# A DeltaNet stage under a list scheduler: 64x64 products of the merges staggered by head, booked times and the order of projections replaced

## The chip, the cores and the metric

The kernel runs on one core of a Trainium2 chip, in one launch. The metric is the device time of the launch in microseconds; a run of the kernel is told as the median of its executions with the lowest and the highest beside it. All arithmetic is in float32. The large products of the dense work are split by the kernel into three products of rounded parts (high times high, low times high, high times low).

## The reference, cut to what matters

The network has two layers on a sequence of 1024 positions of width 1024. The change lies wholly in the first of them, a gated DeltaNet with 8 heads of 128 and chunks of 64:

```python
q, k, v = chunks(q), chunks(k), chunks(v)
gcum = jnp.cumsum(chunks(g[..., None])[..., 0], axis=-1)
decay = jnp.where(causal, jnp.exp(jnp.where(causal, diff, 0.0)), 0.0)
m = jnp.where(strict, jnp.einsum("bhnid,bhnjd->bhnij", k_beta, k) * decay, 0.0)
uw = lax.linalg.triangular_solve(m + eye, rhs, left_side=True, lower=True, unit_diagonal=True)
...
def step(state, inp):
    v_new = u_c - jnp.einsum("bhcd,bhdv->bhcv", w_c, state)
    o_c = jnp.einsum("bhcd,bhdv->bhcv", qd, state) + jnp.einsum("bhcj,bhjv->bhcv", a_c, v_new)
    state = state * dec[..., None, None] + jnp.einsum("bhcd,bhcv->bhdv", ke, v_new)
```

Around it stand the projection of the normed input to q, k, v and the gate z (each 1024 wide), a causal convolution of width 4 with silu on q, k and v, and the output projection with the residual. After it come a gated convolutional FFN, a chunked attention layer and a second FFN.

## The kernel before

**The dense work.** The four projections are 32 tiles of 128 output columns, each for two halves of the sequence (512 positions). One half of one tile is 8 units, and one unit is three matmuls of 128x128 weights on 512 columns, written in `dense` (lines 118, 119 and 120), which accumulate in one PSUM tile `acc`. The output projection is 16 more halves of 8 units (`acco`). A tile's weights come by one DMA (`raw_tile`, line 571) and are split into high and low parts on ScalarE and GpSimd (`split_tile`). After each half `project` takes the convolution's taps on ScalarE and VectorE and silu on ScalarE and GpSimd.

**The recurrence between it.** While TensorE works through the units, the kernel puts the small work of the DeltaNet between them, for the heads in four groups t = 0..3 (heads 0-3 and 4-7 of the first half, then of the second). The kernel works on pairs of chunks, so its blocks are 128x128. `gram` makes k times k (`pg`, line 712) and the masked matrix `mn`; `invert_blocks` inverts its small diagonal blocks on VectorE; `merge` (two calls for each t, each for two heads with four blocks each) puts the inverse of the 128x128 blocks together from them; `prep` makes transposes of k and v and the product `pqk`; `chain` carries the state from block to block (lines 926, 930, 939 on TensorE, a step on VectorE or ScalarE after each), `output` (903, 904) makes the output of a block, `qnorm` takes the sums of squares of q (transposes `pq`, line 655, then four squares on ScalarE, line 659), and `finish` with `turn` or `turn_last` norms and turns the result (`po`, lines 985 and 1032).

**The merge, step by step.** On TensorE a merge before the change is six groups of small products on one PSUM tile `pm` of 128 partitions by 8 by 64 columns: 32 products of 32x32 (line 845), 32 more (851), 16 (862), 24 (872 and 874), then 8 products of 64x64 that write the lower 64 partitions (881), and 8 products of 64x64 that write the upper 64 partitions (886). Between them stand copies on ScalarE or VectorE, among them the copy of `pm` into `TY` after 881 (line 883) and into the inverse `U` after 886 (line 888), each of 64 partitions by 512. The 8 products are four blocks of each of the two heads.

**What sets the order.** TensorE's, VectorE's and ScalarE's instructions stand in the order in which the program text issues them, and class `Flow` decides that order while the kernel is built. Each piece of small work is a generator that yields the booked time from which its next step may be issued. `Flow.T` is a booked clock of TensorE: `pe(n, dt)` adds the booked time of small products, one unit adds 0.69. `on(engine, cost)` books work on VectorE ("D"), ScalarE ("A") or GpSimd ("G") and gives the time at which it is booked to be done. `Flow.run` issues the first ready item by rank whose time plus `slack` (0.5) has passed on the booked clock, and one unit of dense work where there is none. `bank` hands out the two PSUM tiles of the pool `paux` (two buffers), in which `pg`, `pq`, `pk`, `pqk`, `pv`, `pu` and `po` stand in turn: the third user has to wait until the first one has been read out. The list `ORDER` names the sequence in which the tiles of k, q and v are projected. No booked number is in the program that runs; the numbers only decide which instruction follows which.

## Time and profile before

| what | value |
|---|---|
| three executions | 2499.27 us median (2497.41 to 2501.43) |
| profiled execution, span from the first to the last instruction | 2493.3 us |
| granted TensorE clock | 1.000 of full speed |
| TensorE matmul busy, whole span | 2466.1 us (99%), 13785 matmul records |
| VectorE / ScalarE / GpSimd busy | 74% / 58% / 61% |
| the DeltaNet stage with its output projection | about 0 to 671 us of the span |

The profiled execution is known by its span; 6.0 us lie between that span and the median of the three executions, which were timed from outside. A float32 matmul of 128 or fewer columns in the small work stands in the trace as two records, a transposition as one, so "x16" for the 64x64 products is eight products. Records of matmuls overlap (a matmul of 512 columns reads 0.39 us and the next one starts 0.23 us after it), so the time that TensorE gives to a matmul is read from the chain of waits or from the starts in the timeline, not from the busy time. The matmuls' line numbers are those of the kernel before; in the changed kernel most lines lie 3 or 18 lower down.

### The profile page before, as it was taken

The numbers are of one execution on the slowest core, as the hardware profiler recorded it, in microseconds if no ns is written. First come the engines' busy times: TensorE is split into PE (matmuls) and PEld (weight loads), VectorE is DVE, ScalarE is ACT, GpSimd is POOL, SyncE is SP. The second block draws the span as 40 slices with busy tenths as digits, with TensorE's granted clock in tenths as the row PEclk, the third lists the DMA queues.
The fourth block names the chain that finished last, engine by engine and source line by source line (L and its number), as shares of the span: only waits on it lengthen the run. The fifth ranks groups of instructions, "written<-read, shape, count | busy, mean of one in ns | idle before, by whom it ended". The sixth has DMA issues, their size and how long they took to land.

```text
span 2493.3 us, 39279 instructions
## 1 busy us (share of the span) xinstructions
PE 2466.1 (99%) x13785; PEld 2057.0 (83%) x13785; DVE 1842.5 (74%) x2985; ACT 1442.1 (58%) x2770; POOL 1523.0 (61%) x1548
## 2 busy tenths in 40 slices
PE   8999999999999999999999999999999999999998
PEld 6888888888888888888788888888877888888877
DVE  5665874567798888888866656666589788888886
ACT  6444546474465556565555666667456565666555
POOL 3655653357357777777626454455554777778774
PEclk9999999999999999999999999999999999999999
DMA  8734435565347777777841232333444799777788
GB/s 228 188 105 118 142 110 153 156 194 163 96 108 148 150 153 151 153 144 156 183 151 55 67 80 77 81 76 95 145 114 119 184 176 180 166 169 171 152 187 224
DMA packets 383877, 353.19 MB, mean 142 GB/s; under 512 B 97600, under 2 KB 304448, under 8 KB 383680
## 3 DMA queue, kind: packets, MB, share of 16 engines
q1 hardware_dynamic: 350704, 243.46, 34.4%
q0 software_dynamic: 28224, 98.58, 22.5%
q10 hardware_dynamic: 4752, 8.65, 0.9%
q8 instruction: 108, 1.77, 0.3%
q14 instruction: 89, 0.73, 0.1%
HBM read 182.25 MB, written 156.30 MB: 136 GB/s over the span
## 4 chain that ended last, share of the span: by engine, by line
PE 81%; POOL 6%; DVE 4%; issue 4%; DMA 2%; ACT 2%; SPq 0%; ACTq 0%; POOLq 0%; DVEq 0%
PE acc L118 8%; PE pu L1448 8%; PE acc L119 8%; PE acc L120 8%; PE pu L1446 8%; PE pu L1447 8%; PE pd L1448 3%; PE pd L1446 3%; PE pd L1447 3%; POOL ul L1412 3%; PE acco L118 2%; PE acco L120 2%; PE acco L119 2%; PE ptp L2353 2%; PE poT L2399 1%
## 5 line engine op out<-in xcount | busy, mean ns | idle before, releaser
L1412 POOL TENSOR_TENSOR ul<-r,uh 128x512 fp32r<-128x512 f32 x266 | 430.4, 1638 | 258.3 <-ACT uh L1434 253.5
L118 PE MATMUL acc<-xh,whi 128*128 128x512 f32 x896 | 369.3, 413 | 0.5 <-ACT xh L1094 0.5
L119 PE MATMUL acc<-xl,whi 128*128 128x512 f32 x896 | 352.1, 393 | 0.4 <-POOL xl L381 0.3
L120 PE MATMUL acc<-xh,wlo 128*128 128x512 f32 x896 | 351.3, 392 | 0.0
L103 POOL TENSOR_TENSOR wlo<-wraw,whi 128x256 fp32r<-128x256 f32 (+1 forms) x326 | 237.0, 758 | 107.8 <-ACT whi L101 105.3
L1434 ACT CAST uh<-r 128x512 fp32r<-128x512 f32 x289 | 177.1, 623 | 183.3 <-DVE r L1412 148.8
L1448 PE MATMUL pu<-xh,ul 128*128 128x512 f32 x524 | 204.4, 390 | 0.7 <-POOL ul L1412 0.7
L1446 PE MATMUL pu<-xh,uh 128*128 128x512 f32 x524 | 204.4, 390 | 0.7 <-ACT keep L1575 0.7
L1802 ACT COPY stage<-pd 128x1024 f32<-128x1024 f32 x180 | 175.3, 1014 | 49.7 <-PE pd L1448 48.8
L1447 PE MATMUL pu<-xl,uh 128*128 128x512 f32 x524 | 203.9, 389 | 0.0
L120 PEld LDWEIGHTS acc<-xh,wlo 128*128 128x128 f32 x896 | 168.5, 188 | 37.1
L2308 POOL TENSOR_SCALAR sS<-sS,st 128x640 f32<-128x640 f32 (+4 forms) x128 | 87.6, 691 | 178.4 <-DVE st L2306 168.2
L119 PEld LDWEIGHTS acc<-xl,whi 128*128 128x128 f32 x896 | 169.3, 189 | 28.4 <-POOL xl L381 2.5
L118 PEld LDWEIGHTS acc<-xh,whi 128*128 128x128 f32 x896 | 169.1, 189 | 27.5 <-ACT xh L1094 0.9
L1412 POOL TENSOR_TENSOR dl<-a,dh 128x512 fp32r<-128x512 f32 x90 | 153.3, 1703 | 47.4 <-ACT dh L1434 37.2
L1541 DVE SCALAR_TENSOR_TENSOR gate<-gpre,colt,gate 128x1023 f32<-128x1023 f32 (+2 forms) x92 | 176.5, 1919 | 2.5 <-ACT gate L1538 1.8
L1541 DVE SCALAR_TENSOR_TENSOR val<-vpre,colt,val 128x1023 f32<-128x1023 f32 x88 | 149.2, 1696 | 29.3 <-ACT val L1538 29.3
L2298 DVE CUSTOM_DVE_ANT_0 sS<-sc,bt 128x640 f32<-128x640 f32 (+4 forms) x128 | 84.1, 657 | 111.4 <-PE sc L2294 75.9
L1412 DVE TENSOR_TENSOR r<-r,r 128x512 f32<-128x512 f32 x160 | 130.3, 814 | 32.8 <-POOL ul L1412 31.7
L1412 DVE TENSOR_TENSOR el<-val,eh 128x512 fp32r<-128x512 f32 x90 | 85.4, 949 | 43.2 <-ACT eh L1434 43.2
L1448 PEld LDWEIGHTS pu<-xh,ul 128*128 128x128 f32 x524 | 98.4, 188 | 22.8 <-POOL ul L1412 1.4
L1446 PEld LDWEIGHTS pu<-xh,uh 128*128 128x128 f32 x524 | 98.4, 188 | 21.1 <-ACT keep L1575 1.1
(428 smaller groups left out, 7197.9 us busy)
## 6 DMA issues: line engine op xcount, KB each, us to landing
r<-in_f_w_up_dram SPq DMA_DIRECT2D x176, 256.0 KB, 4.5
d_r<-stage POOLq DMA_DIRECT2D x78, 512.0 KB, 8.1
d_c<-stage POOLq DMA_DIRECT2D x70, 512.0 KB, 8.4
a<-in_f_w_down_dram SPq DMA_DIRECT2D x72, 256.0 KB, 2.9
wraw<-in_a_w_in_dram SPq DMA_DIRECT2D x32, 512.0 KB, 4.5
d_e<-stage POOLq DMA_DIRECT2D x32, 512.0 KB, 8.3
wraw<-in_a_w_out_dram SPq DMA_DIRECT2D x16, 512.0 KB, 4.1
d_r<-h ACTq DMA_DIRECT2D x32, 256.0 KB, 2.8
```

The lines of the kernel that those rows point to most:

```text
L103: nc.gpsimd.tensor_tensor(lo[:, c], raw[:, c], hi[:, c].bitcast(F32), op=ALU.subtract)
L118: mm(ps, hi[:, kw, wcol : wcol + P], rh[k][s], start=st, stop=False)
L119: mm(ps, hi[:, kw, wcol : wcol + P], rl[k][s], start=False, stop=False)
L120: mm(ps, lo[:, kw, wcol : wcol + P], rh[k][s], start=False, stop=sp)
L1412: tt = lambda eng, o, a, b, op: eng.tensor_tensor(o, a, b, op=op)
L1434: copy(hi, src)
L1446: mm(ps, w[0][:, cw], x[0], start=first, stop=False, skip_group_check=True)
L1447: mm(ps, w[0][:, cw], x[1], start=False, stop=False, skip_group_check=True)
L1448: mm(ps, w[1][:, cw], x[0], start=False, stop=last, skip_group_check=True)
L1541: nc.vector.scalar_tensor_tensor(t_[:, a:c1], p_[:, a - step : c1 - step], w[:, 2 - step : 3 - step], t_[:, a:c1], op0=ALU.mult, op1=ALU.add)
L1802: nc.scalar.copy(t_, ps)
L2308: nc.gpsimd.tensor_scalar(S, S, st[:, 3:4], 1.0, op0=ALU.mult, op1=ALU.mult)
```

## The change

Three things are changed, all in the DeltaNet stage.

First, the last two groups of a merge become three. The functions `low` and `corner` are the same 64x64 products as before, for one block of one head `a`. Now the first group is `low` of the first head (four products), the second takes `corner` of the first head and `low` of the second in turn (eight products), and the third is `corner` of the second head (four products). `low` reads partitions 0 to 63 and writes partitions 64 to 127 of `pm`; `corner` reads 64 to 127 and writes 0 to 63. The two copies of 64 by 512 on ScalarE become four of 64 by 256. A head is marked merged when its own copy into `U` (in `close`) is booked.

```diff
-            for a, c, n in blocks:
-                mm(pm[64:128, n], mn[a][0:64, c, 64:128], TY[0:64, n], start=True, stop=True)
-            wv.pe(8, 0.12)
-            nc.scalar.copy(TY[64:128], pm[64:128])
-            yield wv.on("A", 0.6)
-            for a, c, n in blocks:
-                mm(pm[0:64, n], TY[64:128, n], U[64:128, n, 64:128], start=True, stop=True)
-            wv.pe(8, 0.12)
-            nc.scalar.copy(U[0:64, :, 64:128], pm[0:64])
-            t_ = wv.on("A", 0.6)
...
+            def low(a, c):
+                mm(pm[64:128, 4 * a + c], mn[a][0:64, c, 64:128], TY[0:64, 4 * a + c], start=True, stop=True)
+
+            def corner(a, c):
+                mm(pm[0:64, 4 * a + c], TY[64:128, 4 * a + c], U[64:128, 4 * a + c, 64:128], start=True, stop=True)
+
+            def close(a):
+                nc.scalar.copy(U[0:64, 4 * a : 4 * a + 4, 64:128], pm[0:64, 4 * a : 4 * a + 4])
+                Us[hds[a], s] = U[:, 4 * a : 4 * a + 4]
+                wv.mark(("merged", hds[a], s), wv.on("A", 0.4))
+
+            for c in range(4):
+                low(0, c)
+            wv.pe(4, 0.134)
+            nc.scalar.copy(TY[64:128, 0:4], pm[64:128, 0:4])
+            yield wv.on("A", 0.4)
+            for c in range(4):
+                corner(0, c)
+                low(1, c)
+            wv.pe(4, 0.14)
+            nc.scalar.copy(TY[64:128, 4:8], pm[64:128, 4:8])
+            t_ = wv.on("A", 0.4)
+            close(0)
+            yield t_
+            for c in range(4):
+                corner(1, c)
+            wv.pe(4, 0.134)
+            close(1)
```

Second, about forty booked times get other values, and the booked clock gets a price for the passage from small products back to dense units (`turnover`, 0.09). A unit is booked at 0.683 and `slack` is 0.6. Some of them:

```diff
+            self.unit, self.turnover, self.mixed = 0.69, 0.0, 0.0
...
         def pe(self, n, dt=0.22):
             self.T += n * dt
+            self.mixed = self.turnover
...
-            self.T += 0.69
+            self.T += self.unit + self.mixed
+            self.mixed = 0.0
...
-            wv.pe(4, 0.11)
+            wv.pe(4, 0.1)
...
-            slot[0] = wv.on("A", 1.9)
+            slot[0] = wv.on("A", 1.62)
...
-            slot[0] = t2_ = wv.on("D", 1.18)
+            slot[0] = t2_ = wv.on("D", 0.69)
...
-        wv.slack = 0.5
+        wv.slack = 0.6
+        wv.unit, wv.turnover = 0.683, 0.09
```

Third, the tiles of k, q and v are projected in another order:

```diff
-        ORDER = [(w[0], int(w[1])) for w in "k2 k0 k1 k3 q2 q0 q1 k5 k4 q3 v0 v1 k6 v2 v3 k7 q4 q5 q6 q7 v5 v4 v6 v7".split()]
+        ORDER = [(w[0], int(w[1])) for w in "k2 k0 k1 k3 k5 k4 q2 q0 q1 v0 v1 k6 v3 k7 v2 q4 q3 v5 q5 v4 q6 q7 v6 v7".split()]
```

Of TensorE's, VectorE's, GpSimd's and SyncE's instructions both programs have the same number (12353 on TensorE), ScalarE has 16 more, the two more copies in each of the eight merges. From the last part of the output projection on, the instructions of every engine stand in the same order in both.

On TensorE the eight merges show the first part. Here is the end of the third merge before (`mn_1565` and `mn_1752` are the matrices of its two heads, `U_3337` its inverse, the rows between are three dense units):

```order
L881 MATMUL pm_3383<-TY_219,mn_1565 64x64 x4
L881 MATMUL pm_3383<-TY_219,mn_1752 64x64 x4
L118 MATMUL acc_3705<-xh3_1_245,whi_3388 128x512
L119 MATMUL acc_3705<-xl3_1_246,whi_3388 128x512
L120 MATMUL acc_3705<-xh3_1_245,wlo_3389 128x512
L118 MATMUL acc_3705<-xh4_1_249,whi_3388 128x512
L119 MATMUL acc_3705<-xl4_1_250,whi_3388 128x512
L120 MATMUL acc_3705<-xh4_1_249,wlo_3389 128x512
L118 MATMUL acc_3705<-xh5_1_253,whi_3388 128x512
L119 MATMUL acc_3705<-xl5_1_254,whi_3388 128x512
L120 MATMUL acc_3705<-xh5_1_253,wlo_3389 128x512
L886 MATMUL pm_3383<-U_3337,TY_219 64x64 x8
```

And here on TensorE the end of the fourth merge of the changed kernel, from within its middle group (L884 is `low` of the second head, L887 `corner`; `U_3565` is the inverse of the pair):

```order
L884 MATMUL pm_3633<-TY_219,mn_2505 64x64
L887 MATMUL pm_3633<-U_3565,TY_219 64x64
L884 MATMUL pm_3633<-TY_219,mn_2505 64x64
L887 MATMUL pm_3633<-U_3565,TY_219 64x64
L884 MATMUL pm_3633<-TY_219,mn_2505 64x64
L118 MATMUL acc_3885<-xh7_1_261,whi_3499 128x512
L119 MATMUL acc_3885<-xl7_1_262,whi_3499 128x512
L120 MATMUL acc_3885<-xh7_1_261,wlo_3500 128x512
L118 MATMUL acc_4024<-xh0_0_231,whi_3819 128x512
L119 MATMUL acc_4024<-xl0_0_232,whi_3819 128x512
L120 MATMUL acc_4024<-xh0_0_231,wlo_3820 128x512
L887 MATMUL pm_3633<-U_3565,TY_219 64x64 x4
```

Two groups of eight with three units between have become groups of four, eight and four; in this merge two units lie between the last two of them, as few as in any of the eight. In all, the stage's small products stand in 198 groups between dense units before and in 207 now.

The second place is on TensorE too, in the middle of the stage, where `qnorm` of several heads comes close together in the two buffers of `paux`. Before (`pq_3420` and `pq_3443` are the transposes of two heads; the next user of `paux` is a third, `pq_3506`, seven dense rows below the last row here):

```order
L655 MATMUL pq_3420<-ident_65,kq_2626 128x128 x4
L118 MATMUL acc_3435<-xh0_1_233,whi_3228 128x512
L119 MATMUL acc_3435<-xl0_1_234,whi_3228 128x512
L120 MATMUL acc_3435<-xh0_1_233,wlo_3229 128x512
L655 MATMUL pq_3443<-ident_65,kq_2332 128x128 x4
L845 MATMUL pm_3383<-T_3381,mn_1565 32x32 x16
L845 MATMUL pm_3383<-T_3381,mn_1752 32x32 x16
L118 MATMUL acc_3435<-xh1_1_237,whi_3228 128x512
L119 MATMUL acc_3435<-xl1_1_238,whi_3228 128x512
L120 MATMUL acc_3435<-xh1_1_237,wlo_3229 128x512
L118 MATMUL acc_3435<-xh2_1_241,whi_3228 128x512
L119 MATMUL acc_3435<-xl2_1_242,whi_3228 128x512
```

On TensorE in the changed kernel (`pq_4114`, `pq_4140` and `pq_4150` belong to three heads, `pc_4111` to the state of a fourth):

```order
L658 MATMUL pq_4114<-ident_65,kq_2390 128x128 x4
L118 MATMUL acc_4024<-xh7_0_259,whi_3819 128x512
L119 MATMUL acc_4024<-xl7_0_260,whi_3819 128x512
L120 MATMUL acc_4024<-xh7_0_259,wlo_3820 128x512
L118 MATMUL acc_4130<-xh0_1_233,whi_3819 128x512
L119 MATMUL acc_4130<-xl0_1_234,whi_3819 128x512
L120 MATMUL acc_4130<-xh0_1_233,wlo_3820 128x512
L948 MATMUL pc_4111<-vv_3585,U_3053 128x128
L658 MATMUL pq_4140<-ident_65,kq_3475 128x128 x4
L658 MATMUL pq_4150<-ident_65,kq_3567 128x128 x4
```

The third of these transposes takes the buffer of the first: before, five units and 32 small products and the second transpose lay between them, now two units, one product of the chain and the second transpose.

More of the change, by code (lines that the diff above doesn't have):

```diff
@@ L575, in split_tile @@
             wt = split_w(raw, [P, KT, P])
-            wv.on("G", 2.75, wv.on("A", 1.0))
+            wv.on("G", 2.9, wv.on("A", 1.04))
             return wt
@@ L620, in taps @@
                         nc.vector.scalar_tensor_tensor(o_, ps[:, 0:n], ca[:, m, 3 - j : 4 - j], o_, op0=ALU.mult, op1=ALU.add)
-                    wv.later(wv.on("D", 2.19), silu)
+                    wv.later(wv.on("D", 2.5), silu)
                 def silu():
@@ L772, in prep @@
             nc.gpsimd.tensor_tensor(q, q, eq, op=ALU.mult)
-            t = max(t, wv.on("G", 1.4))
+            t = max(t, wv.on("G", 1.3))
             yield t1_
@@ L813, in invert_blocks @@
                 column(i)
-                t_ = wv.on("D", 0.4 + 2.2e-3 * i * i)
+                t_ = wv.on("D", 0.33 + 3.0e-3 * i * i)
                 if i % 2 == 0 or i > 8:
@@ L857, in merge @@
                 nc.gpsimd.tensor_copy(U[b[i], :, b[i]], D[b[i]])
-            wv.on("G", 1.37, t_)
+            wv.on("G", 1.7, t_)
             yield t_
@@ L904, in output @@
             mm(po, at[:, q], y, start=c == 0, stop=True)
-            wv.pe(1 + (c > 0))
+            wv.pe(1 + (c > 0), 0.21)
             nc.scalar.copy(vv[:, q], po)
@@ L930, in chain @@
                 mm(pc, U[:, q], vv[:, q], start=True, stop=True)
-                wv.pe(1)
+                wv.pe(1, 0.2)
                 while outs[a] < i - 2:
@@ L939, in chain @@
                     mm(pc, ke[:, q], y, start=True, stop=True)
-                    wv.pe(1)
+                    wv.pe(1, 0.2)
                     while outs[a] < i - 1:
@@ L971, in finish @@
             rsqrt(r, f, t2[:, sl, h2])
-            t_ = wv.on("D", 2.2)
+            t_ = wv.on("D", 2.55)
             for hd, vv in zip(hds, vvs):
@@ L975, in finish @@
                 nc.gpsimd.tensor_tensor(vv, vv, fa, op=ALU.mult)
-                t_ = wv.on("G", 1.82, t_)
+                t_ = wv.on("G", 1.06, t_)
             yield t_
@@ L1032, in turn_last @@
                 nc.tensor.transpose(po[:, cs(c)], vv[:, c], ident)
-            wv.pe(4, 0.11)
+            wv.pe(4, 0.1)
             nc.vector.scalar_tensor_tensor(yt, po, g_o, zt, op0=ALU.mult, op1=ALU.mult)
-            slot[0] = t = wv.on("D", 1.11)
+            slot[0] = t = wv.on("D", 0.74)
             room.append(zt)
@@ L1050, in yz @@
             room.append(zt)
-            yield wv.on("D", 0.56) - wv.slack
+            yield wv.on("D", 0.72) - wv.slack
             yield from wait(("acts", s))
@@ L1057, in split_yt @@
             nc.scalar.copy(acts[0][k][s], yt)
-            t = wv.on("A", 0.34)
+            t = wv.on("A", 0.62)
             e = "D" if k % 2 == 0 else "G"
@@ L1311, in then @@
                 next(its[s])
-                wv.on("D", 0.49, wv.on("A", 0.69))
+                wv.on("D", 0.8, wv.on("A", 0.63))
                 if m == KT - 1:
@@ L1319, in then @@
                         wv.add(1.2, "normed", lambda: t0 + 0.54, tail(its[s]))
-            wv.later(wv.on("D", 0.64), then)
+            wv.later(wv.on("D", 0.69), then)
             yield
```

39 lines of the change are left out of this document (18 added, 21 removed).

## The prediction

> **What bounds the kernel now.** The page comes first, for the span and for the chain that ended last.
>
> ```profile
> span 2493.3 us, 39279 instructions
> PE 2466.1 (99%) x13785; PEld 2057.0 (83%) x13785; DVE 1842.5 (74%) x2985; ACT 1442.1 (58%) x2770; POOL 1523.0 (61%) x1548
> PE 81%; POOL 6%; DVE 4%; issue 4%; DMA 2%; ACT 2%; SPq 0%; ACTq 0%; POOLq 0%; DVEq 0%
> ```
>
> TensorE (PE) is busy 99% of the span and carries 81% of the chain. But an average over the whole kernel says little on one stage, so the busy time by stage comes next (window, length, then busy time of PE, PEld, DVE, ACT, POOL, the granted clock, DMA share and GB/s).
>
> ```profile
> 0.00:47.00 47.00, 38.43 (x181) 26.94 (x181) 26.99 (x47) 32.06 (x58) 17.89 (x33) 1.00 0.82 238
> 47.00:640.00 593.00, 592.57 (x4876) 501.55 (x4877) 375.72 (x986) 309.62 (x842) 329.71 (x435) 1.00 0.52 149
> 640.00:671.00 31.00, 30.00 (x140) 24.45 (x138) 25.75 (x39) 16.11 (x29) 7.44 (x6) 1.00 0.40 106
> 671.00:2493.00 1822.00, 1805.14 (x8592) 1504.06 (x8592) 1414.03 (x1915) 1084.33 (x1842) 1167.93 (x1076) 1.00 0.60 137
> ```
>
> The window from 47 to 640 us is where the scheduler rules, and there TensorE is without a matmul for 593.00 - 592.57 = 0.43 us. The other three engines are busy 52 to 63% of it. Overlapping matmul records can hide a short wait, so the table of waits for TensorE, from 47 to 671 us, is the check (engine, line, releaser: total, times, longest).
>
> ```profile
> PE pss L372 <- DVE nacc L364: 0.6, 1, 0.6
> PE po L985 <- DVE mn L724: 0.2, 1, 0.2
> PE pv L778 <- DMA vv<-d_v: 0.2, 1, 0.2
> ```
>
> Three waits, 1.0 us in all. The first belongs to the norm behind the last output tile, whose instructions stand in the same order in both programs. So the stage lasts as long as TensorE takes to stream its products. A better order of the same products can win the 0.4 us of the other two waits, and whatever short waits the records hide (a rival below). The products' own streaming time changes in the merges alone.
>
> **The merges, part one: the products.** In the chain of waits, overlapping is taken out: a row's second number is the time that passed until the next one took over. Around the third merge it reads (start, us, what):
>
> ```profile
> 315.42 0.62 PE pm L862 x32
> ...
> 317.33 0.89 PE pg L712 x8
> ...
> 323.62 0.23 PE acc L120
> 323.85 1.07 PE pm L881 x16
> 324.92 0.43 PE acc L118
> 325.35 0.23 PE acc L119
> ...
> 327.19 1.07 PE pm L886 x16
> 328.26 1.09 PE pg L712 x8
> 329.35 0.23 PE acc L118
> ```
>
> Eight products of 64x64 take 1.07 us, and the row that follows is 0.20 longer than its like: 0.43 against 0.23 for a dense matmul, 1.09 against 0.89 for `pg`. The 0.20 is the price of leaving such a group. An ordinary group has no such price; the chain a little earlier shows four transposes and the dense matmul behind them:
>
> ```profile
> 309.50 0.44 PE pq L655 x4
> 309.94 0.23 PE acc L118
> ```
>
> So a merge's two groups cost 2 x (1.07 + 0.20) = 2.54 us before. After the change there are three groups, hence one more 0.20. The question is what the groups themselves take. The timeline has three groups of small products (start, busy time, engine, line):
>
> ```profile
> 315.35 0.69 PE L862 MATMUL pm<-T,mn 32*32 32x32 f32 x32
> 305.80 0.75 PE L845 MATMUL pm<-T,mn 32*32 32x32 f32 x64
> 323.78 1.14 PE L881 MATMUL pm<-TY,mn 64*64 64x64 f32 x16
> ```
>
> L862 has 16 products, two for each of eight blocks, on different 32-row parts of the array; L845 has 32, four for each block. Twice the products take 9% longer, so products that read and write different partitions run beside each other, and the time goes by rounds: eight in each of the three groups. The changed merge has 4 + 4 + 4 = 12 rounds in place of 16, if `corner` and `low` overlap as those do. How much of 1.07 goes with the rounds? By the chain, eight rounds of 64 columns take 1.07 and eight of 32 columns (L862) 0.62; drawn down to no columns, 0.17 is left that does not shrink. A group of four rounds is then (1.07 - 0.17) / 2 + 0.17 = 0.62, and a merge 3 x (0.62 + 0.20) = 2.46 us: 0.08 less than before, **0.6 us less for eight merges**. One end is that nothing is fixed: 3 x (0.535 + 0.20) = 2.21, 2.7 us less in all. The other is that the pairs do not overlap at all: 0.62 + 1.07 + 0.62 + 0.60 = 2.91, 3.0 us more in all. I take -0.6, since the two rows with overlap are from the same tile `pm` and the same code. The third group, thus, takes back most of what the overlap gives.
>
> **Part two: the copies.** Two copies become four.
>
> ```profile
> L883 ACT COPY TY<-pm 64x512 f32<-64x512 f32 x8 | 4.7, 582 | 14.0 <-PE pm L881 14.0
> L865 ACT COPY X<-pm 32x256 f32<-32x256 f32 x16 | 5.8, 365 | 7.0 <-PE pm L862 6.9
> ```
>
> A copy of 64x512 takes 0.58 us, one of 256 columns 0.37 by the nearest row; ScalarE gets 4 x 0.37 - 2 x 0.58 = 0.3 us more in each merge, 2.5 us in all, beside 283 us in which it is idle in the window. Behind the first copy the new middle group waits; the order puts at least two units, 6 x 0.23 = 1.4 us, or as much in other products between, more than 0.37 and its start. Cost 0; were the cover gone, 0.4 us a merge. Both heads' chains start later or earlier by a few us, which costs nothing while TensorE has units to fill with, and it has the same 640.
>
> **Part three: the booked times and the order.** Not one of these numbers runs on the chip. The order they give can put a consumer too near to its producer. For the two buffers of `paux` the second place shown above is the closest kind. The timeline of ScalarE shows what reading one `pq` takes (first and last rows of one head's four squares):
>
> ```profile
> 305.06 0.28 ACT L659 ACTIVATE junk<-pq 128x128 f32<-128x128 f32 x1
> ...
> 306.43 0.20 ACT L659 ACTIVATION_READ_ACCUMULATOR junk<-pq 128x1 f32 x1
> ```
>
> That is 306.63 - 305.06 = 1.57 us. In the new order there lie six dense matmuls (6 x 0.23), one chain product (0.22, half of the row of 0.44 for four records) and the second transpose (0.44): 2.04 us, so ScalarE may come 0.47 late. In the old order 15 dense matmuls, 0.44 and a group of 0.68 + 0.20 lay there, 4.8 us: 3.2 to spare. Counted so over all 158 uses of the two buffers, with each group's own evacuation, 11 have less than 0.7 us to spare now and 6 had before. With those 6 the old order waited 0.4 us in all; in proportion I book 0.7 us of waits for the new one and strike the 0.4. The bounds are 0 (every engine is on time) and 11 x 0.6 = 6.6 us, where 0.6 is what is missing when ScalarE has just begun a weight cast, 1.04 less 0.47:
>
> ```profile
> L101 ACT CAST whi<-wraw 128x1024 fp32r<-128x1024 f32 x45 | 47.0, 1044 | 0.0
> wraw<-in_a_w_in_dram SPq DMA_DIRECT2D x28, 512.0 KB, 4.4
> ```
>
> The moved projections take their weight loads along SyncE's queue, past the stores and loads of k, q and v. A load lands 4.4 us after its issue, a tile's 16 units last 16 x 0.69 = 11 us, and the next tile is fetched during the current one; none of TensorE's waits before was for a weight. Cost 0, and if one load were late by a whole landing, 4.4 us once.
>
> **The sum.** -0.6 (merges) - 0.4 (waits that go) + 0.7 (waits that come) = -0.3 us. The profiled span would be 2493.0; the median lies 6.0 above it, so 2499.27 - 0.3 = **2499.0 us**.
>
> **The rivals.**
>
> *The pairs do not overlap.* Then the change to the merges does not do what its order says, and costs 3.0 us: 2499.27 + 3.0 - 0.4 + 0.7 = 2502.6. For it speaks that no row shows 64x64 products in two row halves at once; against it L845. The Trainium skill, "TensorEngine Tiling (Array Packing)", section "Restrictions and Gotchas", says that different row tiles cannot access the same PSUM bank at the same time. Both halves of the middle group write `pm`, so by that rule this rival holds; the trace's rows for L845 and L862, which write one tile `pm` too and overlap, do not agree with it. Chance 0.10.
>
> *The tight hand-overs of `paux` bite.* TensorE stands in front of `pq`, `pg` or `pv` until ScalarE or VectorE has read the buffer, and every unit behind it on TensorE waits along. Each meeting costs up to 0.6 us; it decides from nine of the eleven on, since 0.6 x 9 - 0.6 = 4.8, about 5. All eleven give 2499.27 + 6.6 - 0.6 - 0.4 = 2504.9. For it: `slack` books 0.6 and several read-outs are now booked shorter than before. Against it: ScalarE is busy 309.62 of 593.00, so about half of such meetings find it idle, and the old order's places with equally little to spare cost 0.4 us. Chance 0.10.
>
> *The profile hides waits in the dense matmuls.*
>
> ```profile
> L118 PE MATMUL acc<-xh,whi 128*128 128x512 f32 x485 | 203.9, 420 | 0.0
> L119 PE MATMUL acc<-xl,whi 128*128 128x512 f32 x486 | 189.9, 391 | 0.0
> ```
>
> L118, the first of each unit, reads 29 ns longer than L119: 485 x 0.029 = 14 us. Were that waiting, truer booked times could win half of it: 2499.0 - 7 = 2492. Against it, the row behind `pq` shows 0.23 and the row behind a 64x64 group 0.43: the surplus belongs to the passage from small products, and there are nine more passages now, not fewer. Chance 0.07.
>
> **How the numbers follow.** The forecast, TensorE-bound with a difference of under 3 us, has 0.73. A change of under 0.2%, 5.0 us, cannot be told from none here. The forecast and the rival without overlap (2502.6) both lie within it: 0.83. Faster by more is the hidden-waits rival alone, 0.07; slower by more the hand-overs, 0.10. The range starts from the merges' better end and no new waits, 2499.27 - 2.7 - 0.4 = 2496.2, less 1.2 for the scatter of the runs (the three shown lie up to 2.2 us from their median): 2495.0. It ends with no overlap and 0.7 of waits, 2502.6, plus 0.6 of the same scatter: 2503.2. It leaves out the other two, 0.17.
>
> **What would show it.** In the profile after, TensorE should be without a matmul for less than 2 us between 47 and 640, and its table of waits for that window should hold a few tenths for `pq`, `pv`, `po` or `pg`. In the chain of waits a middle group of a merge (L887 and L884 in turn) should take about 0.6 us and be followed by a row 0.20 longer; 1.07 means no overlap. The first matmul of the FFN should stand at 670 us as before, give or take 3. Wrong would be: waits of TensorE over 5 us in that window, a wait for `whi`, or a stage shorter by over 5 us with all its products at the same pace.

## The result, and the profile after

The changed kernel takes 2528.19 us (2525.92 to 2531.4, four executions), the kernel before 2499.44 us beside it (2497.41 to 2501.43). The ratio is 1.0119, with a 95% interval of 1.0106 to 1.0132: 29 us slower, where 2499.0 had been forecast. The profiled execution took 2529.5 us, 1.7 more than its span; if that holds for the profile before as well, its execution took 2495.0, some 4 us under its median, so differences between the two traces come out larger than those of the medians. From the page after, the span, the engines' busy time and the chain that ended last:

```profile
span 2527.8 us, 39287 instructions
PE 2477.1 (98%) x13785; PEld 2060.8 (82%) x13785; DVE 1855.0 (73%) x2985; ACT 1446.1 (57%) x2786; POOL 1522.8 (60%) x1548
PE 78%; DVE 7%; POOL 5%; issue 4%; ACT 3%; DMA 3%; SPq 0%; ACTq 0%; DVEq 0%; POOLq 0%
```

The matmul records are as many as before, 13785. What TensorE loses on the chain, VectorE, ScalarE and DMA have gained. The busy time by stage (window, length, busy time of PE, PEld, DVE, ACT, POOL, granted clock, DMA share, GB/s) says where:

```profile
47.00:640.00 593.00, 570.61 (x4733) 479.55 (x4734) 366.26 (x960) 300.07 (x840) 300.31 (x400) 0.98 0.50 141
640.00:704.00 64.00, 62.42 (x278) 50.28 (x276) 44.90 (x66) 29.79 (x48) 37.41 (x40) 1.00 0.44 129
704.00:2527.00 1823.00, 1805.71 (x8592) 1503.93 (x8592) 1416.89 (x1914) 1084.12 (x1841) 1166.81 (x1076) 1.00 0.59 137
```

In the window from 47 to 640 us TensorE is without a matmul for 593.00 - 570.61 = 22.4 us, where it was 0.43, and its granted clock is 0.98, where it was 1.00. The rest of the program, from 704 us on, holds the same 8592 matmuls in 1823 us as it held from 671 us on in 1822. So the stage became 33 us longer and nothing else moved. Cut by hundreds, the worst two are these:

```profile
400.00:500.00 100.00, 93.96 (x1009) 82.04 (x1010) 51.38 (x168) 48.04 (x158) 30.95 (x44) 0.98 0.48 137
500.00:600.00 100.00, 89.19 (x896) 74.29 (x896) 41.61 (x96) 54.42 (x142) 45.43 (x51) 0.93 0.49 146
```

The table of waits for TensorE from 47 to 700 us (engine, line, releaser: total, times, longest) names what it stood for:

```profile
PE pc L957 <- ACT y L953: 4.7, 2, 2.9
PE pm L887 <- ACT U L890: 4.6, 1, 4.6
PE acco L120 <- POOL wlo L103: 3.2, 2, 3.0
PE pq L658 <- DMA kq<-d_kq: 1.8, 1, 1.8
PE pm L848 <- DVE T L844: 1.8, 1, 1.8
PE pm L865 <- issue: 1.5, 1, 1.5
...
PE po L1003 <- DVE at L772: 0.6, 1, 0.6
```

All rows of that table add up to 22.8 us; in the same window of the kernel before they added up to 2.8. These are seventeen waits; the releasers are three engines and a load, and one wait names none. The hand-overs of `paux`, from which I expected 0.7 us and for which a rival allowed 6.6, are the small ones: `po` behind the read-out of `at` (0.6), and two more of 0.4 and 0.3 us.

**One wait followed back.** Chain of waits around the longest (start, us, what):

```profile
524.34 5.40 DMA spare<-d_z
...
529.76 0.63 ACT spare L1065
...
530.41 0.37 ACT TY L903
...
530.79 0.38 ACT U L890
...
531.21 1.11 PE pm L887 x8
...
535.04 0.43 PE acc L118
...
538.26 0.23 PE acc L118
```

TensorE wants the last group of a merge (L887). That needs the copies of the merge on ScalarE (L903, L890), 0.37 us each. But on ScalarE, whose instructions run in the order in which they are written, silu of a gate tile (L1065) stands ahead of them, and its input is still on its way: the load lands at 529.74. The timeline of ScalarE has its idle time in front of that silu, 6.20 us:

```profile
529.76 0.63 ACT L1065 ACTIVATE spare<-spare 128x512 f32<-128x512 f32 x1 [6.20 <-DMA spare<-d_z]
```

The load itself left late. Ahead of it in SyncE's queue stands a weight load of the output projection (L1307), which may go only when ScalarE and GpSimd have read the buffer that it overwrites. The waits of SyncE from 517 to 526 us:

```profile
SPq L1307 <- POOL wlo L103: 3.8, 1, 3.8
SPq L1307 <- ACT whi L101: 2.1, 1, 2.1
```

So a weight load that waits for its buffer holds the load of the gate tile, that load holds ScalarE, ScalarE holds the merge, and the merge holds TensorE with every dense unit behind it. And something follows that no row of the kernel before shows: the four products (eight records) take 1.11 us in place of 0.60, and the dense matmuls 0.43 in place of 0.23, until 538.0. The busy time by windows over the same place gives the reason:

```profile
520.00:526.40 6.40, 6.40 (x54) 4.88 (x53) 4.81 (x7) 2.23 (x4) 4.55 (x5) 1.00 0.35 99
526.40:531.10 4.70, 0.18 (x1) 0.00 (x0) 0.68 (x1) 1.31 (x4) 0.00 (x0) 1.00 1.00 335
531.10:538.00 6.90, 6.74 (x28) 5.87 (x29) 2.00 (x5) 2.47 (x8) 0.00 (x0) 0.51 0.66 214
538.00:545.00 7.00, 7.00 (x164) 5.80 (x163) 1.72 (x6) 3.32 (x9) 0.08 (x1) 1.00 0.11 41
```

TensorE idles for 4.5 us in the second window, and through the third its granted clock is halved (0.51). The idle time is paid once, and half of the next 6.9 us as well. (What shows that the halved clock follows from waits stands under "What one wait costs" and in the last section.)

Three other long waits go back to transfers too. From the chains of waits there:

```profile
281.00 5.71 DMA d_y<-yo
...
286.71 1.03 ACT whi L101
...
287.74 0.28 ACT y L953
...
395.94 5.02 DMA D<-d_u
...
436.89 8.16 DMA kq<-d_kq
```

At 281 it is a store: the tile that ScalarE writes next (`th`) shares its buffers with `yo` and comes free only when `yo` has been written out; ScalarE stands for it, and a weight cast and then `y` come late. At 396 the diagonal blocks of a merge are loaded and VectorE's transpose waits (then `pm` L848), at 437 the `kq` of a head (then `pq` L658).

**The account.** The trace's clock records show the clock at half from 288.7, 445.8, 572.0 and 582.3 us for 3.4 us each and from 531.1 for 6.8: 20.4 us. The profile of the kernel before has none in this stage. The waits are 22.8 - 2.8 = 20.0 us more, half the clock over 20.4 us costs 10.2: 30.2 us, where the median rose by 28.8 and the stage in the trace grew by 32.8.

### The profile page after: what moved, and what is told of

Read it like the earlier page. It is cut to its first block, busy times and chain, and to the rows that moved or that the text cites. A ratio compares the mean times of both kernels' runs of the same rounds, so it can differ in the third digit from the quotient of the medians.

```text
span 2527.8 us, 39287 instructions
## 1 busy us (share of the span) xinstructions
PE 2477.1 (98%) x13785; PEld 2060.8 (82%) x13785; DVE 1855.0 (73%) x2985; ACT 1446.1 (57%) x2786; POOL 1522.8 (60%) x1548
## 4 chain that ended last, share of the span: by engine, by line
PE 78%; DVE 7%; POOL 5%; issue 4%; ACT 3%; DMA 3%; SPq 0%; ACTq 0%; DVEq 0%; POOLq 0%
PE pu L1467 9%; PE pu L1465 8%; PE pu L1466 8%; PE acc L118 7%; PE acc L119 7%; PE acc L120 7%; PE pd L1466 4%; PE pd L1465 4%; PE pd L1467 4%; PE ptp L2372 2%; PE acco L120 2%; PE acco L118 2%; PE acco L119 2%; POOL ul L1431 2%; PE poT L2418 1%
## 5 line engine op out<-in xcount | busy, mean ns | idle before, releaser
L118 PEld LDWEIGHTS acc<-xh,whi 128*128 128x128 f32 x896 | 169.6, 189 | 26.9 <-ACT xh L1112 0.8
```

The source lines that it names most:

```text
L118: mm(ps, hi[:, kw, wcol : wcol + P], rh[k][s], start=st, stop=False)
```

## The experiments

Sixteen kernels ran, each compared with runs of the kernel before on the same chip (medians 2497.95 to 2500.36). Two theories recur in the texts. **A**: loads land later than booked because SyncE's queue stands behind stores and weight loads, so moving those or booking loads longer gives the time back. **E**: nearly any other order of the same products draws waits of its own, and the order before is one with hardly any. Other letters belong to the texts in which they stand.

### The three parts apart

The first three kernels are the kernel before with one part of the change each, three more have two parts; the diff of each part is shown ahead of the prediction. `e1_merge_only`:

```diff
-            for a, c, n in blocks:
-                mm(pm[64:128, n], mn[a][0:64, c, 64:128], TY[0:64, n], start=True, stop=True)
+            for c in range(4):
+                low(0, c)
```

> Only the last two groups of each merge become three; the old booked times elsewhere and the old order of projections stay. Theory A (waits of TensorE come from loads and read-outs that arrive later than booked in the new sequence; the merges themselves are not to blame): between 2496 and 2504 us, waits of TensorE under 3 us between 47 and 670 us. Rival B (the third group and the two more copies on ScalarE put themselves into the way): over 2510 us, with waits on the copies into TY and U.

Measured: 2514.25 us (2512.03 to 2516.19), ratio 1.0063 (1.0040 to 1.0086). TensorE's largest waits:

```profile
PE pv L778 <- DMA vv<-d_v: 3.1, 1, 3.1
PE acco L120 <- POOL wlo L103: 2.6, 2, 2.3
```

Both texts miss: the time is far above A's 2504, but no wait of the table is on the copies into `TY` and `U`, as B would have it.

`e2_order_only`:

```diff
-        ORDER = [... "k2 k0 k1 k3 q2 q0 q1 k5 k4 q3 v0 v1 ..."]
+        ORDER = [... "k2 k0 k1 k3 k5 k4 q2 q0 q1 v0 v1 k6 ..."]
```

> Only the list of projections is the new one; booked times and merges are the old ones. Theory A1 (the order of projections is what brings consumers and late loads together): over 2515 us. Rival C (the booked times are what does it): within 6 us of 2499.

Measured: 2523.11 us (2521.26 to 2524.95), ratio 1.0098 (1.0069 to 1.0128). Its largest waits of TensorE are others than with the merges alone:

```profile
PE pc L930 <- DVE vv L928: 5.2, 1, 5.2
PE pm L845 <- DVE T L841: 2.8, 1, 2.8
```

`e3_times_only` (booked times, `turnover` and `slack`):

```diff
-        wv.slack = 0.5
+        wv.slack = 0.6
+        wv.unit, wv.turnover = 0.683, 0.09
```

> Only the booked times, the price of a passage and the slack are the new ones; merges and order of projections are the old ones. Rival C (several read-outs are booked shorter than before, and consumers move too near to their producers): over 2515 us. Theory A1: within 6 us of 2499, since the order of projections is the old one.

Measured: 2508.22 us (2504.24 to 2510.82), ratio 1.0038 (1.0027 to 1.0049). Both texts miss: it is more than 6 us above 2499 and under 2515.

`e4_times_order` has the old merges, `e12_times_merges` the old order of projections, `e13_merge_order` the old booked times; each is the changed kernel with one part undone:

```diff
-            for c in range(4):
-                low(0, c)
+            for a, c, n in blocks:
+                mm(pm[64:128, n], mn[a][0:64, c, 64:128], TY[0:64, n], start=True, stop=True)
```

> New booked times and new order of projections, merges as before. Theory A: 2520 to 2536 us, as the full change, since the merges are not to blame. Rival B (merges): within 8 us of 2499.

Measured: 2525.24 us (2522.73 to 2527.75), ratio 1.0107 (1.0077 to 1.0136).

```diff
-        ORDER = [... "k2 k0 k1 k3 k5 k4 q2 q0 q1 v0 v1 k6 ..."]
+        ORDER = [... "k2 k0 k1 k3 q2 q0 q1 k5 k4 q3 v0 v1 ..."]
```

> The full change without its new order of projections: new booked times and staggered merges, old list. If the parts simply add (times 10, merges 16): about 2524 us. If each part only draws another order with its own waits (theory E): anywhere from 2503 to 2528, not the sum. If the list of projections is the harmful part: under 2510.

Measured: 2512.41 us (2508.55 to 2517.04), ratio 1.0050 (1.0028 to 1.0072).

```diff
-        wv.slack = 0.6
-        wv.unit, wv.turnover = 0.683, 0.09
+        wv.slack = 0.5
```

> The kernel before with the staggered merges and the new order of projections, and the old booked times: the last corner between the three parts. If the parts' losses add, merges alone (16 us) and order alone (25 us) give 2499 + 41 = 2540. If each combination is a new arrangement with its own waits, and the order of projections decides how tight it is, it lands between 2514 and 2530, as the four others with the new order that keep the queues as they are, and its waits of TensorE from 47 to 700 us are 12 to 25 us.

Measured: 2526.89 us (2524.22 to 2528.3), ratio 1.0115 (1.0101 to 1.0129).

What follows: every part alone costs time, and the parts do not add. By the medians less those of the kernel before, alone they cost 15.9, 24.8 and 9.9 us, 51 in all, and together 28.8. The new order of projections, put in with the rest unchanged, costs 24.8 (alone), 28.9 - 15.9 = 13.0 (with the merges), 26.9 - 9.9 = 17.0 (with the times) and 28.8 - 12.1 = 16.7 us (with both): always the largest part. The merges cost 15.9 us alone, but 2 to 4 on top of the times, of the order or of both; the times 9.9 alone, and between -3.8 and 2.1 on top of another part. Some of these kernels ran only two to five times, with intervals of 3 to 7 us to each side, so the 13 to 25 us of the order are clear of that scatter and the 2 to 4 and the -3.8 to 2.1 are not. Each kernel has its own list of waits, and the longest of one is mostly not found in the next. One wait does come again in all four of these kernels that have the new order: between 401 and 410 us VectorE waits for the load `D<-d_u`, and `pm` waits for VectorE's `T`, for 1.8 us in the change and 2.8, 6.4 and 3.0 in `e2`, `e4` and `e13`. None of the kernels with the old order has it.

### Moving transfers to another queue

`e5_stores_pool`: the changed kernel with the stores of q, k and v and of the masked matrix issued by GpSimd; TensorE's, VectorE's and ScalarE's instructions stay in the changed kernel's order.

```diff
-                        nc.sync.dma_start(out=store[s], in_=d)
+                        nc.gpsimd.dma_start(out=store[s], in_=d)
...
-                nc.sync.dma_start(out=d_ms[t][i].rearrange("c b j i -> (b j) c i"), in_=cm)
+                nc.gpsimd.dma_start(out=d_ms[t][i].rearrange("c b j i -> (b j) c i"), in_=cm)
```

> The changed kernel with its stores of projected k, q and v and of the small matrices issued by GpSimd, which makes their data, in place of SyncE's queue; TensorE's, VectorE's and ScalarE's orders are the same row for row. Theory A (loads come late because SyncE's queue stands behind stores that wait for GpSimd): waits of TensorE fall from 23 to under 12 us, the time to under 2515. Rival D (VectorE, ScalarE and GpSimd are late by their own work, the loads are not what matters): within 5 us of 2528, or above it by GpSimd's added issues.

Measured: 2524.61 us (2519.99 to 2529.24), ratio 1.0106 (1.0059 to 1.0152). From its table of waits for TensorE:

```profile
PE pc L957 <- ACT y L953: 5.1, 2, 3.4
PE pm L887 <- ACT U L890: 4.6, 1, 4.6
...
PE po L1003 <- POOL vv L993: 1.8, 1, 1.8
```

The wait of `pm` L848 is gone, as A has it, but the two largest stay and others come or grow (`po`): no gain that can be told from two runs.

`e6_stores_weights_pool` moves the weight loads to GpSimd as well:

```diff
-            nc.sync.dma_start(out=raw, in_=a_w_in[:, c0 : c0 + P].rearrange("(k p) m -> p k m", p=P))
+            nc.gpsimd.dma_start(out=raw, in_=a_w_in[:, c0 : c0 + P].rearrange("(k p) m -> p k m", p=P))
```

> As the run before, and the weight loads of the stage are issued by GpSimd as well, so that SyncE's queue no longer stands behind a weight buffer that is still being read. Theory A: under 2510 us. Rival D: 2523 us or more; GpSimd issues some 44 loads more.

Measured: 2538.78 us (2536.3 to 2541.26), ratio 1.0162 (1.0133 to 1.0192). A new wait at the first tiles alone is larger than any before:

```profile
PE acc L118 <- DVE kq L623: 9.1, 1, 9.1
```

The wait of `pm` L887, which a weight load in SyncE's queue had begun, is 1.3 us here in place of 4.6, as that chain has it; but the waits of the whole stage have grown to 32.9 us.

`e9_loads_act`: the changed kernel with the loads of `d_y`, `d_z` and `d_kq` issued by ScalarE.

```diff
-            nc.sync.dma_start(out=yt, in_=d_y[k][s])
+            nc.scalar.dma_start(out=yt, in_=d_y[k][s])
...
-            nc.sync.dma_start(out=zt, in_=d_z[k][s])
+            nc.scalar.dma_start(out=zt, in_=d_z[k][s])
```

> The changed kernel with the loads of the stored z, of the first output halves and of the stored k and q issued by ScalarE at the place where the program text issues them, in place of SyncE's queue, where the trace has them up to 7 us behind that place. TensorE's and VectorE's orders are the same row for row, ScalarE's has 44 issues more. Theory A (loads that leave SyncE's queue late): the waits of 4.6, 3.1 and 1.8 us behind these loads go, their half-clock stretches with them, 2508 to 2518 us. Rival D (ScalarE itself is the late one): no better than 2524, since ScalarE gets more to do.

Measured: 2538.63 us (2538.05 to 2539.21), ratio 1.0153 (1.0124 to 1.0183). The longest wait of TensorE:

```profile
PE pm L875 <- ACT X L868: 7.5, 1, 7.5
```

Now ScalarE itself stands where SyncE stood: it does no work for 10.8 us up to 515.75, in which it issues these loads, and a merge step waits 7.5 us for its copy. In these runs moving transfers only chose whose queue was held. A, as "SyncE's queue is the cause of the loss", falls, though it names the cause of single waits.

### Booking loads longer

`e10_long_loads`: the changed kernel, each booked load 3 us longer; `e14_long_loads6`: 6 us longer; `e15_old_order_long_loads`: 3 us longer with the old order of projections. One of six such lines:

```diff
-            yield wv.T + 5.0
+            yield wv.T + 8.0
```

> The changed kernel with every load of the recurrence booked 3 us longer than now (8.0 in place of 5.0 and so on), so that the scheduler places the consumers later. Theory A: most waits go, under 2512 us. Rival E (any order other than the one before has such waits by chance): 2512 to 2530, with waits at other places.

> The changed kernel with every booked load 6 us longer than booked in it (three more than in the run with 3). Theory of late loads: with 3 us the time fell from 2525 to 2514 and the waits from 22.8 to 14.0 us; 3 more cover the lateness of up to 7 us seen for spare<-d_z, so waits under 9 us, half-clock stretches of at most one, 2502 to 2509. Theory of the draw: the result does not follow the size of the booking; 2510 to 2530, with other waits than with 3.

> The changed kernel with the old order of projections and every booked load 3 us longer. With the old order alone it took 2512.4 (waits 12.7 us). Theory of late loads: the same share goes as with the new order, so about half of 13, 2504 to 2507, waits about 7 us. Theory of the draw: 2502 to 2518, and no wait of the run with the old order is found again.

Measured: 2514.38 us (2513.25 to 2516.75, ratio 1.0061, 1.0038 to 1.0084) with 3 us, 2515.82 (2511.99 to 2517.22, ratio 1.0070, 1.0058 to 1.0083) with 6. With the old order and 3 us it is 2514.9 (2514.47 to 2519.15, ratio 1.0072, 1.0059 to 1.0084), where the old order alone gave 2512.4. In the table of waits for TensorE, this row leads with 6 us on the new order:

```profile
PE pm L887 <- ACT U L890: 2.7, 2, 1.8
```

No single wait there is above 1.8 us. With 3 us on the old order, these two lead:

```profile
PE pv L781 <- DMA vv<-d_v: 5.1, 1, 5.1
PE pq L658 <- ACT junk L662: 3.0, 1, 3.0
```

Three us of booking take back half of the loss on the new order, and the wait for `D<-d_u` near 401 us is gone with 3 and with 6: that fits loads that land later than booked. But the time does not follow the dose, 6 us give no more, and on the old order there is no gain. Each booking also makes another order, so these runs do not tell how much of the gain is the booking and how much the draw. (The kernel whose time fell took 2528 us, not the 2525 of the second text.)

### Small steps away from the kernel before

`e7_before_slack` sets `slack` to 0.55, `e11_swap_two` swaps two neighbours in the old order of projections:

```diff
-        wv.slack = 0.5
+        wv.slack = 0.55
```

> The kernel before with one number changed, the slack 0.55 in place of 0.5; it moves rows in a part of the order only. Theory E (the order before is a rare one without waits, nearly any other order of the same work has them): 2504 to 2525 us, with new waits of TensorE in the moved part. Rival F (orders of this scheduler mostly run without waits, and each of the three changed parts harms by itself): within 4 us of 2499.

Measured: 2501.26 us (2498.91 to 2504.16), ratio 1.0011 (0.9999 to 1.0022), which is not clear of no difference, with waits of 5.3 us and no half clock.

```diff
-        ORDER = [... "... k5 k4 q3 v0 v1 ..."]
+        ORDER = [... "... k5 k4 v0 q3 v1 ..."]
```

> The kernel before with two neighbours of the list of projections swapped (v0 before q3); booked times and merges are the old ones. Theory E (the order before is a rare one without waits): 2508 to 2525 us. Rival F (orders near it run as well): within 5 us of 2499.

Measured: 2505.97 us (2502.87 to 2507.46), ratio 1.0022 (1.0010 to 1.0033), waits of 6.5 us, one half-clock stretch of 3.4. So E, that nearly any other order costs as much as the change, falls in that strength: a small step draws 2 to 6 us, a part of the change 10 to 25. F, within 4 or 5 us of 2499, holds for `e7` and misses in `e11`. None of the kernels came under the kernel before.

### What one wait costs

The copy of head 0's state after its first block is made 12 times on VectorE in `e8_before_late12` and 24 times in `e16_before_late24`, in the kernel before; the values stay the same.

```diff
-                        nc.vector.tensor_copy(Sn, pc)
+                        for _ in range(12 if hd == 0 else 1):
+                            nc.vector.tensor_copy(Sn, pc)
```

> The kernel before with one step of one head made late on purpose: a copy of the state of head 0 after its first block is done 12 times on VectorE, 11 more of 0.2 to 0.28 us, and TensorE has some 1.4 us to spare there. Nothing else changes. If a wait costs what it lasts: 1 to 2 us more than before. If a wait also halves the granted clock for a while afterwards, as in the changed kernel: 3 to 5 us more, with a stretch at half clock behind it.

> The kernel before, in which the copy of head 0's state after its first block is made 24 times on VectorE instead of 12 (and of once), so that one wait of TensorE grows from 2.1 us by 12 x 0.32 = 3.8 to 5.9 us; the result is the same values. If a wait costs itself alone: 2499 + 5.9 = 2505. If each wait of about 2 us or more also halves the granted clock behind it for one or two stretches of 3.4 us: 2507 to 2509.

Measured: 2502.29 us (2501.18 to 2505.44, ratio 1.0013, 1.0002 to 1.0024) and 2506.51 us (2504.56 to 2509.61, ratio 1.0037, 1.0023 to 1.0051). The wait with 12 copies, from its table of waits for TensorE:

```profile
PE pc L926 <- DVE S L948: 2.1, 1, 2.1
```

The same wait with 24 copies:

```profile
PE pc L926 <- DVE S L948: 6.0, 1, 6.0
```

And busy time by windows of the second, through its wait and behind it:

```profile
176.00:183.40 7.40, 5.74 (x178) 4.47 (x169) 6.21 (x17) 3.80 (x9) 3.45 (x6) 1.00 0.32 94
183.40:197.10 13.70, 9.33 (x71) 7.69 (x72) 5.05 (x17) 3.60 (x9) 2.78 (x4) 0.50 0.16 41
197.10:204.00 6.90, 6.90 (x65) 6.14 (x64) 4.14 (x7) 2.25 (x6) 1.84 (x2) 1.00 0.35 118
```

The wait of 6.0 us brings 13.7 us of halved clock, in 9.3 of which TensorE works: 6.0 + 9.3 / 2 = 10.7, with a rise of 8.6 us in the median (5.7 to 12.7 by the interval) and 11.5 in the span. The wait of 2.1 us brings 3.4 us at half: 2.1 + 1.7 = 3.8, where the median rose by 3.6 (0.5 to 6.0). The intervals alone would allow that a wait costs no more than itself; the clock records and the traces do not. In the profile of the second, the FFN's matmul that waits for `keep`, at 671.24 us in the profile before, starts 10.4 us later. In that of the first it starts 5.6 us later, and there a wait of 1.7 us with no releaser stands beside the 3.8. By this account a wait costs about 1.8 times its length, while the medians give 1.7 and 1.4; TensorE's order is that of the kernel before, row for row.

### All runs in one account

"Waits" is the sum of TensorE's table from 47 to 700 us less the 2.8 us of before; "half" the halved-clock time of the same window.

| run | median less before | waits | half / 2 | sum |
|---|---|---|---|---|
| the change | 28.8 | 20.0 | 10.2 | 30.2 |
| e1 merges | 15.9 | 8.9 | 6.8 | 15.7 |
| e2 order | 24.8 | 14.8 | 12.0 | 26.8 |
| e3 times | 9.9 | 5.3 | 3.4 | 8.7 |
| e4 times, order | 26.9 | 18.0 | 8.5 | 26.5 |
| e12 times, merges | 12.1 | 9.9 | 3.4 | 13.3 |
| e13 merges, order | 28.9 | 19.1 | 15.4 | 34.5 |
| e5 stores | 25.9 | 20.9 | 8.5 | 29.4 |
| e6 stores, weights | 40.1 | 30.1 | 11.9 | 42.0 |
| e9 loads on ScalarE | 38.3 | 26.5 | 15.4 | 41.9 |
| e10 loads + 3 | 14.0 | 11.2 | 1.7 | 12.9 |
| e14 loads + 6 | 17.9 | 8.6 | 5.1 | 13.7 |
| e15 old order, loads + 3 | 17.0 | 10.6 | 12.0 | 22.6 |
| e7 slack | 2.5 | 2.5 | 0.0 | 2.5 |
| e11 swap | 5.6 | 3.7 | 1.7 | 5.4 |
| e8 12 copies | 3.6 | 3.1 | 1.7 | 4.8 |
| e16 24 copies | 8.6 | 5.3 | 6.8 | 12.1 |

In all seventeen the sum meets the median within 6 us, in eleven within 2. It is too high where part of a halved stretch lies in a wait itself (4.4 us in e16), and the profiled execution is not the median one. Taken inside each profile, the account is tighter: the time in which TensorE has no matmul, from 47 us to that matmul of the FFN, plus half of the halved time in which it works, gives 32.2 us more than before for the change, and the matmul starts 32.8 us later. The two agree within 3.5 us in sixteen of the seventeen and within 5.5 in e6. So waits and the clock account for nearly all of the loss; at full clock no product became slower. What stays open is why this order of projections draws more waits than the old one whatever stands beside it. The recurring wait for `D<-d_u` is one piece of it. The waits of 400 to 600 us, where recurrence of both halves and the last projections meet, hold most of them in the change (16.8 of 22.8 us), but no run separates the cause there.

## Why the prediction was wrong

**What bounds the stage** held for before and not for after. "So the stage lasts as long as TensorE takes to stream its products" and "it has the same 640" were read from a trace in which the order was already without waits (1.0 us). They describe that order, not the products: TensorE's program still has 12353 instructions, and a product takes the same time where the clock is full.

**The merges** were right, down to the sizes. Chain of waits after, one merge:

```profile
169.30 0.60 PE pm L884 x8
169.90 0.43 PE acc L118
...
171.49 0.20 PE pm L887
171.69 0.05 PE pm L887
...
172.10 0.43 PE acc L118
...
174.59 0.60 PE pm L887 x8
175.20 1.09 PE pqk L770 x8
```

A group of four takes 0.60 (0.62 forecast), the middle group of eight 172.10 - 171.49 = 0.61 (0.62 forecast), and the row behind a group is 0.20 longer (0.43 for a dense matmul, 1.09 for `pqk`): 0.60 + 0.61 + 0.60 + 3 x 0.20 = 2.41 us for this merge, with 2.46 forecast and 2.54 before. Of the 24 groups of the eight merges 22 take 0.60 or 0.61 us; the others are one of 0.70 and the one at 531, at half the clock. So the rival without overlap is false, by which the middle group would have taken 1.07. The Trainium skill, "TensorEngine Tiling (Array Packing)", section "Restrictions and Gotchas", states that different row tiles cannot access the same PSUM bank at once; this trace does not agree with it. The step was sized well, and it decided nothing: put in alone, the new merges cost 15.9 us. They book other times, the scheduler then puts other work at other places behind them, and the waits of that run are at such work, none at the 64x64 products.

**The copies**, "Cost 0": their length was right (0.37 for L903 and L890 in the chain above), but the cover was not. I weighed ScalarE by its idle share, 283 us in the window, and asked only whether 1.4 us of other work lay between copy and consumer. For 6.2 us up to 529.8 ScalarE was idle and yet not to be had: the instruction at the head of its queue waited for a load. Idle time of an engine that runs its queue in order was no cover.

**The term that failed** is "in proportion I book 0.7 us of waits for the new one and strike the 0.4". It should have been 20 us. Three things were wrong in it. I counted only the 158 uses of `paux`, whose hand-overs measured 1.3 us in all; the waits are for loads, for ScalarE and VectorE behind loads, and for GpSimd's weight parts. I scaled the new order by the old one's 0.4 us, the one arrangement in which such places happened to cost almost nothing; and half of that 0.4, the row `pv` behind `vv<-d_v`, is a wait for a load and no hand-over. And I priced a meeting at the consumer's own shortfall, up to 0.6 us, where the price is set by whatever stands ahead in the producer's queue: 4.6 us at 531.

**The moved loads**, "Cost 0, and if one load were late by a whole landing, 4.4 us once": right in kind, wrong in number. A weight's low part from GpSimd was waited for twice, 3.2 us, and four of the long waits begin with some other transfer of 5 to 8 us. The prediction asked of the weight loads whether they would come in time, not what they hold up behind them in SyncE's queue, and of the loads of y, z, `kq` and `D` it asked nothing.

**The clock** was no term at all: 10.2 us of the 30.2. The profile before has no wait above 0.6 us in this stage, and I took the granted clock of 1.00 for a constant.

**The rivals.** The hand-overs of `paux`, 2504.9 with a chance of 0.10, had the right sign and the wrong mechanism: 1.3 us of theirs, not 6.6. The hidden waits in the dense matmuls (2492) found no support: where the clock is full, the dense row behind a group of 64x64 products is still 0.43 and the others 0.23. **What would show it** worked: over 5 us of waits in that window was named as the sign of a wrong forecast, and the FFN's matmul behind `keep`, which I had taken for its first, stands at 704.02 in the chain of waits, 32.8 us later than its 671.24 before.

A range built on the bounds of each counted term was too narrow because the largest term was not counted. Two of the parts alone moved the time by 16 and 25 us; a range that leaves room for another order's own waits would have reached 2530.

## What to carry to other kernels

When a schedule that keeps the critical engine without waits is rearranged, the new order's waits are not those of the old one scaled: ask what each load's issue stands behind, follow the load to the engine that consumes it, and ask what else stands behind it in that engine's queue. By these runs, price a wait of TensorE above some 2 us at half as much again to twice its length. An order that measures without waits is worth keeping as it is; here a changed booking, a changed order and even a shorter merge each cost more than they could have won.

## What the runs showed of the hardware

**The halved clock.** All halved stretches between 47 and 700 us last 3.4 us or a multiple of it, and within an execution their starts lie on one grid: 288.7 and 445.8 in the kernel after are 46 steps of 3.413 us apart, 445.8 and 531.1 are 25. Counted by those grid windows over the changed kernel and the fifteen experiments that have such stretches, from starts and ends of matmul records: at full clock, a window with 2.0 us or more without a matmul was followed by a halved one in 25 of 25 cases, one with 1.5 to 2.0 us in 16 of 28, one with 1.0 to 1.5 in 3 of 25, one with 0.5 to 1.0 in 3 of 78, and one with less in none of 2802. These counts are from 47 to 700 us. So a wait of 2.1 us that falls into one window was always enough, and one of 1.8 us may leave the clock full, as that of `pm` L848 at 401 us does in the kernel after. A halved stretch can also outlast the wait: in `e16` the clock stays at half for two more windows in which TensorE is never idle. The Trainium skill, "TensorE: Matmul & The Clock Gate", "Part 1: The HAM clock gate", has the half clock and a free-running window of about 3.4 us, with which the grid agrees; its rule of no gaps above 3.4 us is too lenient for these traces.

**Waits that name no one.** In a run of small products TensorE sometimes stands with nothing shown as its releaser: 1.5 us before `pm` L865 in the kernel after, and 4.1 us in `e13_merge_order`, from its table of waits:

```profile
PE pc L954 <- issue: 4.1, 1, 4.1
```

The kernel before has none of these, while `e8_before_late12`, with its order and the repeated copies, has one of 1.7 us far behind them. What they are stays open.
